# Moving operands that begin 12 bytes into their tiles, in a one-core decoder trunk

## The chip, the cores and the metric

The kernel runs on one core of a Trainium2 chip. The metric is the time of one execution on the device, in microseconds (us); lower is better. Before the change the median of three runs is 2180.16 us (2179.63 to 2182.27).

A core has TensorE (PE in the profile; PEld is its loading of weights), VectorE (DVE), ScalarE (ACT), GpSimd (POOL) and SyncE (SP), which here only issues transfers. A matmul has a stationary operand, the weights, which are loaded into the array first, and a moving operand, whose columns then stream through it.

## The reference

One layer of a decoder for 512 prompt tokens and 8 sample tokens, 520 columns in all, in fp32:

```
proj = rmsnorm(x) @ w_in            # 2048 -> 6160
mixer = [ short convolution of 3 taps, gated | 4 heads of gated linear attention ]
x = x + mixer @ w_out               # 2048 -> 2048
u, v = split(rmsnorm(x) @ w_up)     # 2048 -> 2 * 5632
x = x + (silu(conv3(u) + b) * v) @ w_down
y = rmsnorm(x)
```

The outputs are y for both kinds of token, the last rows of the convolutions and the states of the attention.

## The kernel before

Activations lie transposed: a tile has 128 features in its 128 partitions and the T = 520 tokens along the row. `halves(t)` cuts it into two moving operands of HT = 260 columns. The large products are computed in float32r, in parts that take a number apart: `hi` is the rounded value, `lo` what the rounding left. ScalarE makes `hi` and VectorE `lo`, for the activations (`split`, lines 121 to 124) and for the weights (`parts`, line 111, and `prepare`, lines 1179 to 1198). A product is three matmuls: hi by hi, hi by the activations' lo, lo by hi.

Three places issue nearly all matmuls:

- `mm3`, line 140, in the first stage (the input projection, tile by tile in `group` and `span`) and at the very end (the last four row tiles of `w_down`, where the columns are cut into 264 and 256 instead of 260 and 260);
- `up_product`, line 1218, for the rest of the input projection and for the FFN's up projection;
- `chunk_product`, line 1461, for `w_out` and `w_down`.

The last two use a scheme that makes a 2 by 2 block product from seven products instead of eight (`ORDER`, seven forms of the activations in `xq` and `xd`, and sums of weights made by VectorE and by accumulating transfers). Each of the seven has 24 matmuls of 260 columns, and 168 matmuls make one group. The loop at line 1668 goes through all products in order, prepares the weights two products ahead, and runs the steps of the gates, norms and stores by due times written into generators (`yield 4.5`: four and a half products later). `InOrder` ties every engine to the order in which the program is written.

The moving operands live in tiles of [128, 520] float32r, 2,080 bytes a row:

- `pair_tiles` (line 200) makes hi and lo tiles: the first stage's `xa`, form 1 of the FFN, and the last activations of `load_last` (line 1436);
- `load_form` (line 630) loads the seven forms of a chunk from DRAM, through SyncE's or GpSimd's queue;
- `form` (line 670) makes the FFN's forms on the chip; `load_sum` (line 1570) loads some of their sums.

Slots are named by tags, and tiles of other kinds share them: `place` in `mixer_sums` (line 699) and the sums `acc` (`new_sums`, line 1420).

Three more kinds of tile matter for the room in SBUF. `tmp` (line 92) gives eight temporaries of T + 2 columns. `keep_last` (line 582) collects the last rows of the convolutions into `last`, [128, 10, n] with n = 8 for the mixer and 11 for the FFN under two tags, transposes them and copies the result to `flat`, from which ten small transfers store them; `flat` has two buffers. `zpad` holds the convolutions' inputs with two columns of padding.

Of the kernel before, what the change touches and what calls it, by code (L numbers as in the profile page):

```python
# [9 lines left out]
F32 = mybir.dt.float32  # L10
F32R = mybir.dt.float32r
# [6 lines left out]
P = 128  # L18
# [4 lines left out]
T = NP + NS  # L23
# [14 lines left out]
def trunk_kernel(  # L38
# [13 lines left out]
    tp = ctx.enter_context(tc.tile_pool(name="tmp", bufs=8))  # L52
# [37 lines left out]
                self.last[i.engine] = i.name  # L90

    def tmp():
        return tp.tile([P, T + 2], F32, tag="t", name="t")

    def two(ap):
        return ap.rearrange("p (a b) -> p a b", a=2)
# [24 lines left out]
    def split(src, hi, lo, scale=None):  # L121
        if scale is None:
            nc.scalar.activation(hi, src, AF.Copy)
            nc.vector.tensor_tensor(lo, src, hi.bitcast(F32), op=ALU.subtract)  # L124
        else:
            nc.scalar.activation(hi, src, AF.Copy, scale=scale)
            nc.vector.scalar_tensor_tensor(
                lo, src, scale, hi.bitcast(F32), op0=ALU.mult, op1=ALU.subtract
            )

    def halves(t):
        return t[:, :HT], t[:, HT:T]
# [63 lines left out]
    bigA = actx.enter_context(tc.tile_pool(name="bigA", bufs=1, side="right"))  # L196
    bctx = ctx.enter_context(ExitStack())
    b12p = bctx.enter_context(tc.tile_pool(name="b12", bufs=1))

    def pair_tiles(pool, tag):  # L200

        return [pool.tile([P, T], F32R, tag=f"{tag[0]}{s}{tag[1:]}", name=tag[0] + s) for s in "hl"]

    xa, xw = [], {}
    for k in range(KD):
# [71 lines left out]
    with ExitStack() as es:  # L277
# [173 lines left out]
        for k in range(KD):  # L451
            c, t = k // 4, k % 4
# [117 lines left out]
    zp = actx.enter_context(tc.tile_pool(name="zpads", bufs=1, side="right"))  # L570
    yt1 = actx.enter_context(tc.tile_pool(name="yt1", bufs=1, side="right"))
# [4 lines left out]
    last = [None]  # L576
# [5 lines left out]
    def keep_last(z, j, n, new_p, new_s, get=None):  # L582

        jj = j % n
        if jj == 0:
            last[0] = zp.tile([P, 10, n], F32, tag=f"last{n}", name="last", bufs=2)
        if get:
            nc.scalar.activation(last[0][:, :, jj], z[:, NP:], AF.Copy)
        else:
            nc.gpsimd.tensor_copy(last[0][:, :, jj], z[:, NP:])  # L590
        if jj == n - 1:
            lt, c0 = last[0], (j - n + 1) * P

            def out():
                ps = (get or bank)()
                nc.tensor.transpose(
                    ps[: 10 * n, :P], lt.rearrange("p r j -> p (r j)"), idn
                )
                flat = zp.tile([110, P], F32, tag="flat", name="flat", bufs=2)
                nc.scalar.activation(flat[: 10 * n, :], ps[: 10 * n, :P], AF.Copy)  # L600
                for r in range(10):
                    dst = new_p[0, 0, r] if r < 2 else new_s[0, r - 2, 1]
                    (nc.gpsimd if get else nc.sync).dma_start(
                        dst[c0 : c0 + n * P].rearrange("(j p) -> j p", p=P),
                        flat[r * n : (r + 1) * n, :],
                    )

            soon.append(lambda: None)
            soon.append(out)

    def minus(out, ps, x):
        nc.vector.scalar_tensor_tensor(out, ps, -1.0, x, op0=ALU.mult, op1=ALU.subtract)
# [4 lines left out]
    def sub(out, x, y):  # L617
        nc.vector.tensor_tensor(out, x, y, op=ALU.subtract)
# [8 lines left out]
    slots = [None] * KD  # L627
    forms_d, xd = {"wo": g_d}, {}

    def load_form(kind, c, j):  # L630

        home = (7 * c + j) % 8
        if kind == "down" and home in (0, 7):
            home = 7 - home
        parts_ = []
        for x in range(2):
            tiles = []
            for q in range(2):
                t = slots[2 * home + q].tile(
                    [P, T], F32R, tag=f"y{'hl'[x]}{2 * home + q}", name="form"  # L640
                )
                pool = x == 1 if c == 0 else kind == "wo"
                (nc.gpsimd if pool else nc.sync).dma_start(
                    two(t.bitcast(F32)),
                    forms_d[kind][c][PLACE[ORDER[j]], x, 2 * q : 2 * q + 2].rearrange(
                        "i p c -> p i c"
                    ),
                )
                tiles += halves(t)
            parts_.append(tiles)  # L650
        xd[kind, c, ORDER[j]] = list(zip(*parts_))
# [11 lines left out]
    def acc_tag(n):  # L663
        return f"x{'hl'[n % 2]}{8 + n // 2}"
# [5 lines left out]
    def form(f, g):  # L670

        if f == 1:
            x = pair_tiles(bigA, f"b{g}")
        elif f in (2, 3):
            x = [
                bigA.tile([P, T], F32R, tag=acc_tag(4 * g + q), name="b2")
                for q in ((0, 3) if f == 2 else (1, 2))
            ]
        else:
            k = homes.get((f, g), {5: 0, 4: 4, 6: 8, 7: 12}[f] + g)  # L680
            x = [slots[k].tile([P, T], F32R, tag=f"y{s}{k}", name=f"y{s}{k}") for s in "hl"]
        for j, q in enumerate(zip(*(halves(y) for y in x))):
            xq[f, 2 * g + j] = q
        return x

    def first_tile(kind, g, m):

        return 4 * g + 2 * m if kind == "down" else 2 * g + 8 * m

    def rows_of(d, kind, g, q):  # L690

        m, b = first_tile(kind, g, q // 2), q % 2
        return d[m : m + 2, :, b * HT : (b + 1) * HT].rearrange("m p c -> p m c")

    def mixer_sums():

        def place(n):
            return yt1.tile([P, T], F32, tag=f"y{n}", name="yx")  # L700

        for g in (1, 2, 3, 0):
            xg = [place(n) for n in ("l0 h8 l8 h0" if g % 2 else "l1 l4 h4 h0").split()]
            for q, x in enumerate(xg):
                nc.sync.dma_start(two(x), rows_of(xT_d, "mix", g, q))
            yield
            for q, x in enumerate(xg):
                m = first_tile("mix", g, q // 2)
                for j, h in enumerate(halves(x)):
                    nc.scalar.activation(h, h, AF.Copy, scale=gmix[:, m + j : m + j + 1])  # L710
                if q == 1:
                    yield
            yield
            t1, t3, t4, b22 = xg
            t2 = place("h1")
            sub(t1, t1, t3)
            minus(t2, t1, b22)
            yield
            if g:
                for f, t in ((5, t1), (4, t2)):  # L720
                    nc.gpsimd.dma_start(mt_d[f - 4, g], t)
            sub(t3, b22, t3)
            minus(t4, t2, t4)
            yield
            nc.gpsimd.dma_start(mt_d[3, g], t4)
            if g:
                nc.gpsimd.dma_start(mt_d[2, g], t3)
        for f, t in ((5, t1), (6, t3), (4, t2)):
            split(t, *form(f, 0))
# [32 lines left out]
    with ExitStack() as mix:  # L762
# [44 lines left out]
        with ExitStack() as gl:  # L807
# [263 lines left out]
            for h in range(NH):  # L1071
# [3 lines left out]
                k = gp.tile([P, T], F32, tag="qk", name="k", bufs=5)  # L1075
# [3 lines left out]
                q = gp.tile([P, T], F32, tag="qk", name="q", bufs=5)  # L1079
# [6 lines left out]
                for d in range(2):  # L1086
                    ps = group(w_in, 4096 + h * DV + d * P, xa, None if h + d else v0)
                    t = gp.tile([P, T], F32, tag="v", name="v", bufs=2)
# [330 lines left out]

    def new_sums(g):  # L1420
        for q in range(4):
            acc[g, q] = bigA.tile([P, T], F32, tag=acc_tag(4 * g + q), name="acc")

    def load_residual(g):

# [21 lines left out]
    acc, dnp = {}, [None, None]  # L1447
# [55 lines left out]
    def projected(g):  # L1503
# [25 lines left out]
        def out(f, t):  # L1529

            if f == 7 or g == NG - 1:
                split(t, *form(f, g))
            else:
                nc.sync.dma_start(t_d[f - 4, g], t)
# [133 lines left out]
    for i, (kind, at, r) in enumerate(order):  # L1668
        j, n = i % 7, i // 7
# [41 lines left out]
        if i in (0, 2, NW, NW + 2):  # L1711

            x = xq[1, 0][0]
# [11 lines left out]
        if kind == "wo":  # L1725
            c, g = at
            if c == 0 and g == 2 and j == 0:
                load_form("wo", 1, 0)
            if c == 0 and j == 4 and g + 1 < NG:
                load_residual(g + 1)  # L1730
            if c == 0 and g == 2 and j == 1:
                add_residual("wo", 0)
            if c == 0 and g == NG - 1 and j >= 1:
                load_form("wo", 1, j)
            if c == 1 and g == NG - 1:

                for f, h in {
                    0: ((5, 0), (5, 1)), 2: ((5, 2),), 3: ((4, 0), (4, 1)), 4: ((4, 2),),
                    5: ((6, 0), (6, 1)), 6: ((6, 2),),
                }.get(j, ()):  # L1740
                    loaded.append(load_sum(t_d, f, h))
        if 7 * n in (NM - 7, NU - 7):
            for x in {1: (0, 1), 2: (2, 3), 4: (4, 5), 6: (6,)}.get(j, ()):
                load_form(groups[n + 1][0], 0, x)
        if i == NM:
            new_sums(0)
        if kind == "down":
            c, g = at
# [157 lines left out]
```

## Time and profile before

| | us |
|---|---|
| median of the runs before | 2180.16 |
| span of the profiled execution | 2180.4 |
| PE busy | 2152.9 (99%), 17,751 matmuls |
| PEld busy | 2131.3 (98%) |
| DVE busy | 1735.7 (80%) |
| ACT busy | 1114.0 (51%) |
| POOL busy | 438.1 (20%) |
| moved by DMA | 415.51 MB, mean 191 GB/s |
| mean granted TensorE clock | 0.995 |

The profiled execution's own time is its span, 2180.4 us, 0.2 us over the median. Matmuls are pipelined: one takes some 283 ns from its start to its modelled end, while the next starts much sooner. Sums of busy time therefore overlap, and it is the number of matmuls that start in a stretch which tells their pace. A line "A:B length, busy (xcount) ..." is a stretch of time with each engine's busy time and count.

### The profile page before, as it was taken

What the parts mean: (1) busy time and instruction counts of PE and PEld (TensorE: products, weight loads), DVE (VectorE), ACT (ScalarE), POOL (GpSimd) and SP (SyncE); (2) the same over time, 40 slices, a digit from 0 to 9 for tenths busy, and PEclk for the clock granted to TensorE, in tenths of its full rate; (3) what the DMA queues carried; (4) which work ended last, traced back from release to release, by engine and by line L of the source; (5) the groups of instructions that cost most, each with busy time, mean ns of one, the idle gap of its engine ahead of it and who ended that gap; (6) DMA issues with size and microseconds to landing.
All of it is one profiled execution on the core that took longest, in us unless ns stands there. A gap on an engine that the chain in (4) does not pass through costs nothing.

```text
span 2180.4 us, 43803 instructions
## 1 busy us (share of the span) xinstructions
PE 2152.9 (99%) x17751; PEld 2131.3 (98%) x17751; DVE 1735.7 (80%) x2298; ACT 1114.0 (51%) x1625; POOL 438.1 (20%) x625
## 2 busy tenths in 40 slices
PE   9999999999999999999999999999999999999997
PEld 8999999999999999999999999999999999999997
DVE  6346465578888897988888988998998778888886
ACT  6335435355544586555555555555555553444445
POOL 4213131121243321121221131122111310010000
PEclk9999999999999999999999999999999999999999
DMA  8545464387788996667676676676677886894734
GB/s 247 147 125 158 122 191 124 92 246 210 204 257 248 297 266 176 179 178 187 164 189 174 165 195 176 163 194 177 171 186 190 285 202 197 248 271 132 226 107 156
DMA packets 467163, 415.51 MB, mean 191 GB/s; under 512 B 21641, under 2 KB 426393, under 8 KB 466817
## 3 DMA queue, kind: packets, MB, share of 16 engines
q1 hardware_dynamic: 424081, 289.71, 46.5%
q0 software_dynamic: 42832, 122.93, 21.4%
q8 instruction: 139, 2.28, 0.4%
q14 instruction: 63, 0.52, 0.1%
q10 hardware_dynamic: 48, 0.07, 0.0%
HBM read 299.45 MB, written 80.31 MB: 174 GB/s over the span
## 4 chain that ended last, share of the span: by engine, by line
PE 88%; DMA 4%; DVE 3%; issue 1%; ACT 1%; POOL 1%; SPq 0%; ACTq 0%; DVEq 0%; POOLq 0%
PE mm L1218 34%; PE mm L140 16%; PE ms L1218 14%; PE y L1461 7%; PE x L1461 7%; PE f L1461 3%; PE e L1461 3%; PE ms L957 1%; DMA raw<-in_w_out_dram 1%; DMA form<-g_d 1%; DVE lo L1198 1%; DMA g_d<-fh 1%; DMA x_d<-acc 1%; DMA yl<-t_d 0%; DMA raw<-in_w_down_dram 0%
## 5 line engine op out<-in xcount | busy, mean ns | idle before, releaser
L1218 PE MATMUL mm<-yl,hi 128*128 128x260 f32 x1696 | 479.8, 283 | 3.6 <-DVE yl L124 3.6
L1218 PE MATMUL mm<-yh,hi 128*128 128x260 f32 x1696 | 480.5, 283 | 2.1 <-ACT ms L1228 1.8
L1218 PE MATMUL mm<-yh,lo 128*128 128x260 f32 x1696 | 479.8, 283 | 0.8 <-DVE lo L1198 0.8
L1194 ACT ACTIVATE hi<-raw 128x1024 fp32r<-128x1024 f32 x324 | 342.6, 1057 | 233.9 <-PE mm L1218 69.0
L1198 DVE TENSOR_TENSOR lo<-raw,hi 128x1024 fp32r<-128x1024 f32 x324 | 395.2, 1220 | 41.2 <-ACT hi L1194 40.7
L1198 DVE TENSOR_TENSOR lo<-s,hi 128x1024 fp32r<-128x1024 f32 x243 | 298.3, 1228 | 127.2 <-ACT hi L1194 121.9
L1194 ACT ACTIVATE hi<-s 128x1024 fp32r<-128x1024 f32 x243 | 256.9, 1057 | 217.2 <-DVE s L1139 80.2
L1218 PEld LDWEIGHTS mm<-yl,hi 128*128 128x128 f32 x1696 | 320.1, 189 | 4.2 <-DVE yl L124 4.2
L1218 PEld LDWEIGHTS mm<-yh,hi 128*128 128x128 f32 x1696 | 319.7, 189 | 2.7 <-ACT ms L1228 2.0
L1218 PEld LDWEIGHTS mm<-yh,lo 128*128 128x128 f32 x1696 | 320.4, 189 | 1.2 <-DVE lo L1198 1.2
L1218 PE MATMUL ms<-b,hi 128*128 128x260 f32 x1408 | 257.8, 283 | 0.0
L1218 PEld LDWEIGHTS ms<-b,hi 128*128 128x128 f32 x1408 | 218.5, 190 | 0.0
L1461 PE MATMUL x<-form,hi 128*128 128x260 f32 x1120 | 204.6, 283 | 0.8 <-DVE acc L1480 0.8
L1461 PE MATMUL y<-form,hi 128*128 128x260 f32 x1120 | 204.5, 282 | 0.5 <-DVE acc L1480 0.5
L1139 DVE TENSOR_TENSOR s<-s,raw 128x1024 f32<-128x1024 f32 x162 | 197.8, 1221 | 2.8
L1218 PE MATMUL ms<-b,lo 128*128 128x260 f32 x704 | 199.5, 283 | 0.0
L1461 PEld LDWEIGHTS x<-form,hi 128*128 128x128 f32 x1120 | 172.4, 188 | 1.2 <-issue 1.0
L1461 PEld LDWEIGHTS y<-form,hi 128*128 128x128 f32 x1120 | 172.5, 188 | 0.8 <-issue 0.7
L1461 PE MATMUL y<-form,lo 128*128 128x260 f32 x560 | 158.2, 283 | 0.8 <-DVE lo L1198 0.8
L1461 PE MATMUL x<-form,lo 128*128 128x260 f32 x560 | 158.1, 282 | 0.0
L112 DVE TENSOR_TENSOR lo<-raw,hi 128x1024 fp32r<-128x1024 f32 x76 | 93.7, 1238 | 78.2 <-ACT hi L111 71.6
L1218 PEld LDWEIGHTS ms<-b,lo 128*128 128x128 f32 x704 | 133.4, 190 | 0.0
(366 smaller groups left out, 5077.8 us busy)
## 6 DMA issues: line engine op xcount, KB each, us to landing
raw<-in_w_up_dram SPq DMA_DIRECT2D x176, 512.0 KB, 4.7
raw<-in_w_down_dram SPq DMA_DIRECT2D x96, 512.0 KB, 5.5
raw<-in_w_in_dram SPq DMA_DIRECT2D x92, 512.0 KB, 4.4
form<-f_d SPq DMA_DIRECT2D x126, 260.0 KB, 6.8
raw<-raw POOLq DMA_DIRECT2D x56, 512.0 KB, 5.5
f_d<-t POOLq DMA_DIRECT2D x80, 260.0 KB, 5.5
raw<-in_w_out_dram SPq DMA_DIRECT2D x32, 512.0 KB, 12.7
form<-g_d POOLq DMA_DIRECT2D x42, 260.0 KB, 7.7
```

The source lines that it names most:

```text
L112: nc.vector.tensor_tensor(lo, raw, hi.bitcast(F32), op=ALU.subtract)
L140: nc.tensor.matmul(o, w, xx, start=first and i == 0, stop=last and i == 2)
L957: nc.tensor.matmul(pb[:, c * 64 : (c + 1) * 64], L[:, c, :], rhs[:, c], start=True, stop=True,)
L1139: return lambda: nc.vector.tensor_tensor(out, x, y, op=ALU.add)
L1194: nc.scalar.activation(his[i], src, AF.Copy)
L1198: nc.vector.tensor_tensor(los[i], src, his[i].bitcast(F32), op=ALU.subtract)
L1218: nc.tensor.matmul(st["bank"][b], w[:, k, :], x, start=b not in st["used"] and k == 0 and j == 0, stop=k == 7 and j == 2, skip_group_check ...
L1461: nc.tensor.matmul(ps[:, m, :], w[:, k, m * P : (m + 1) * P], x, start=b not in st["used"] and k == 0 and j == 0, stop=k == 3 and j == 2, ...
```

## The change

A new helper `moving` makes a tile of T + 3 = 523 columns and returns it from column 3 on: the operand has 520 columns as before and begins 12 bytes into its tile. `pair_tiles`, `load_form` and `form` take their tiles from it. `place` and `new_sums`, which share the slots, make tiles of the same width and use the first 520 columns. To make room for three more columns per tile, `tmp` loses its two spare columns, `last` uses one tag of 110 columns for both sizes, and `flat` has one buffer. The instructions, their order and the transfers' shapes stay; the weights' tiles stay as they are.

```diff
     def tmp():
-        return tp.tile([P, T + 2], F32, tag="t", name="t")
+        return tp.tile([P, T], F32, tag="t", name="t")
...
+    def moving(pool, tag, name):
+
+        return pool.tile([P, T + 3], F32R, tag=tag, name=name)[:, 3:]
+
     def pair_tiles(pool, tag):
 
-        return [pool.tile([P, T], F32R, tag=f"{tag[0]}{s}{tag[1:]}", name=tag[0] + s) for s in "hl"]
+        return [
+            moving(pool, f"{tag[0]}{s}{tag[1:]}", tag[0] + s) for s in "hl"
+        ]
...
-            last[0] = zp.tile([P, 10, n], F32, tag=f"last{n}", name="last", bufs=2)
+            last[0] = zp.tile([P, 110], F32, tag="last", name="last", bufs=2)[:, : 10 * n]
+            last[0] = last[0].rearrange("p (r j) -> p r j", j=n)
...
-                flat = zp.tile([110, P], F32, tag="flat", name="flat", bufs=2)
+                flat = zp.tile([110, P], F32, tag="flat", name="flat", bufs=1)
...
-                t = slots[2 * home + q].tile(
-                    [P, T], F32R, tag=f"y{'hl'[x]}{2 * home + q}", name="form"
-                )
+                t = moving(slots[2 * home + q], f"y{'hl'[x]}{2 * home + q}", "form")
...
-                bigA.tile([P, T], F32R, tag=acc_tag(4 * g + q), name="b2")
+                moving(bigA, acc_tag(4 * g + q), "b2")
...
-            x = [slots[k].tile([P, T], F32R, tag=f"y{s}{k}", name=f"y{s}{k}") for s in "hl"]
+            x = [moving(slots[k], f"y{s}{k}", f"y{s}{k}") for s in "hl"]
...
-            return yt1.tile([P, T], F32, tag=f"y{n}", name="yx")
+            return yt1.tile([P, T + 3], F32, tag=f"y{n}", name="yx")[:, :T]
...
-            acc[g, q] = bigA.tile([P, T], F32, tag=acc_tag(4 * g + q), name="acc")
+            acc[g, q] = bigA.tile([P, T + 3], F32, tag=acc_tag(4 * g + q), name="acc")[:, :T]
```

## The prediction

> **What bounds the kernel now.** I read the page's first part, then the chain that ended last, then the matmul count per stretch, and last single matmuls in order of time.
>
> ```profile
> span 2180.4 us, 43803 instructions
> PE 2152.9 (99%) x17751; PEld 2131.3 (98%) x17751; DVE 1735.7 (80%) x2298; ACT 1114.0 (51%) x1625; POOL 438.1 (20%) x625
> ...
> PE 88%; DMA 4%; DVE 3%; issue 1%; ACT 1%; POOL 1%; SPq 0%; ACTq 0%; DVEq 0%; POOLq 0%
> ```
>
> TensorE is busy for 99% of the span and makes 88% of the chain. Busy alone says little, because one matmul overlaps the next. The distance from one start to the next is what counts, and the view of stretches gives it (columns: length; busy time and count of PE, PEld, DVE, ACT, POOL; clock; DMA share; GB/s):
>
> ```profile
> 600.00:700.00 100.00, 100.00 (x836) 100.00 (x836) 84.11 (x99) 48.90 (x65) 39.48 (x55) 1.00 0.86 251
> ...
> 1000.00:1100.00 100.00, 100.00 (x837) 100.00 (x837) 89.80 (x124) 55.25 (x82) 23.89 (x37) 1.00 0.67 174
> ...
> 2000.00:2100.00 100.00, 100.00 (x837) 100.00 (x837) 83.90 (x86) 42.08 (x45) 0.00 (x0) 1.00 0.52 159
> ```
>
> About two of the 837 stick out at the edges, so 835 start in 100 us: **0.1198 us apart**. It is the same with GpSimd at 39 us or at none and with the DMA share at 0.86 or at 0.52, at a full clock. So other engines and transfers don't set this pace; it is TensorE's own. Where it isn't kept is the passage into the FFN:
>
> ```profile
> 700.00:760.00 60.00, 60.00 (x500) 59.82 (x499) 50.74 (x55) 32.69 (x44) 25.44 (x35) 1.00 1.00 292
> 760.00:830.00 70.00, 64.17 (x501) 62.64 (x500) 66.83 (x83) 54.73 (x89) 12.59 (x16) 0.96 1.04 275
> ```
>
> There the DMA share is 1.00 and more, and between 760 and 830 us some 83 matmuls are missing against the pace (70 / 0.1198 = 584).
>
> How many matmuls does the change touch? Those of lines 140, 1218 and 1461 read the tiles that are moved:
>
> ```profile
> 0.00:2181.00 2181.00, 1074.78 (x8904) 0.99 0.68 191
> ...
> 0.00:2181.00 2181.00, 566.05 (x4704) 0.99 0.68 191
> ...
> 0.00:2181.00 2181.00, 426.22 (x3264) 0.99 0.68 191
> ```
>
> Together 8,904 + 4,704 + 3,264 = 16,872 of the 17,751. At 0.1198 us they make 2,021 us of the span, so **one nanosecond per matmul is worth 16.9 us**, 0.8%.
>
> **Is there anything to win in the 119.8 ns?** Four stretches of the order in time bear on it. Of plain fp32, with the same 260 columns (line 550), then 64 columns (line 957):
>
> ```profile
> 166.67 1.04 PE L550 MATMUL ms<-t,ones 128*128 128x260 f32 x4
> 133.43 1.00 PE L957 MATMUL ms<-L 128*128 128x64 f32 x8
> ```
>
> And how long one of each lasts (the mean in ns stands ahead of the idle time):
>
> ```profile
> L550 PE MATMUL ms<-t,ones 128*128 128x260 f32 x16 | 4.2, 382 | 0.0
> L957 PE MATMUL ms<-L 128*128 128x64 f32 x224 | 28.3, 269 | 1.0 <-DVE L L897 1.0
> ```
>
> One lasts 0.38 us at line 550 and 0.27 at line 957. So four starts at line 550 are (1.04 - 0.38) / 3 = 0.220 us apart. If float32r streams columns at twice that rate (an estimate, from 0.220 against 0.1198), its pass would need 0.110. The 64-column passes are (1.00 - 0.27) / 7 = 0.104 apart though they have a quarter of the columns, so what sets them is loading 128 columns of weights. Both bounds lie near 0.110 us; the kernel's pass takes 0.1198. **Some 9.8 ns per matmul are unexplained** by columns or by weights alone; they appear when both streams run at full rate. In time the two begin together:
>
> ```profile
> 1000.06 0.28 PE L1218 MATMUL mm<-yh,hi 128*128 128x260 f32 x1
> 1000.07 0.19 PEld L1218 LDWEIGHTS mm<-yl,hi 128*128 128x128 f32 x1
> ```
>
> Then the number of columns. At the end the batch is cut into 264 and 256 columns (first and last rows; 24 rows and 22 rows in all):
>
> ```profile
> 2112.62 0.28 PE L140 MATMUL mm<-bh,hi 128*128 128x264 f32 x1
> ...
> 2115.43 0.28 PE L140 MATMUL mm<-bh,lo 128*128 128x264 f32 x1
> ```
>
> ```profile
> 2149.03 0.28 PE L140 MATMUL mm<-bl,hi 128*128 128x256 f32 x1
> ...
> 2151.50 0.28 PE L140 MATMUL mm<-bl,hi 128*128 128x256 f32 x1
> ```
>
> 2.81 / 23 = 0.1222 us for 264, 2.47 / 21 = 0.1176 for 256, 0.1198 for 260 between: 4.6 ns for eight columns, more than a bare column time (0.110 / 260 x 8 = 3.4). The surplus grows with what is read. Four columns are 16 bytes; per 16 bytes the pass costs 119.8 / 65 = **1.84 ns**. I use that as the step in which a start can shift things.
>
> Last, does the start matter? A tile is 2,080 bytes and its second half begins 1,040 bytes in, so in a pool's line of tiles the halves begin alternately at a multiple of 32 bytes and 16 past it. Line 1461 takes six matmuls from one half, then six from the next:
>
> ```profile
> 2040.77 0.40 PE L1461 MATMUL e<-form,hi 128*128 128x260 f32 x2
> ...
> 2041.49 0.40 PE L1461 MATMUL e<-form,hi 128*128 128x260 f32 x2
> ...
> 2042.20 0.40 PE L1461 MATMUL e<-form,hi 128*128 128x260 f32 x2
> ...
> 2042.92 0.40 PE L1461 MATMUL e<-form,hi 128*128 128x260 f32 x2
> ```
>
> 0.72, 0.71 and 0.72 us: a start moved by 16 bytes changes nothing to 0.01 us in six, 1.7 ns in one. By the widths in the code, every operand of these three lines begins at a multiple of 16 bytes. The change puts all of them at 12 bytes past one, which no row shows.
>
> **The change part by part.**
>
> (1) The start of the moving operand, 16,872 times. From below: a gain cannot exceed the surplus, 119.8 - 110 = 9.8 ns each, 165 us. From above: a pass of 1,040 bytes that starts 12 bytes into a line touches 66 lines of 16 bytes where it touched 65; a line more at 1.84 ns is 31.0 us. Between these ends I take a gain, because the surplus is there, it appears only with two reads at full rate, and all starts, weights (slices of 512 bytes) and moving columns alike, now fall on the same 16-byte grid at the same instant (the two rows at 1000.06). Three columns of four move the columns' line changes away from those of the weights. Of its size I take one step of the grid, 1.84 ns, not the whole surplus, since the nearest row, the 16-byte shift, shows nothing and the two reads drift against each other when one is held up. 16,872 x 1.84 = 31.0 us.
>
> (2) The stretch 700 to 830 us waits for transfers; its 1,001 matmuls give nothing: 1,001 x 1.84 = 1.8 us less. **Sum: -29.2 us.**
>
> (3) Writers of the wider tiles. ScalarE and VectorE write the same elements 12 bytes further on. I cost that at nothing: VectorE is busy 89.8 of 100 us in the densest stretch and TensorE waits for neither there. A pass of 0.1180 instead of 0.1198 raises VectorE to 91% (89.8 x 0.1198 / 0.1180); with the whole surplus gone it would stand at 98% and begin to bind.
>
> (4) Transfers into the wider tiles (`load_form`, `load_sum`, `load_last`) land 12 bytes into a tile, in the same pieces. Those that the chain shows waited for are
>
> ```profile
> 712.37 7.03 DMA form<-g_d
> 719.91 7.50 DMA form<-g_d
> ...
> 809.67 10.59 DMA yl<-t_d
> ```
>
> 25.1 us in all; elsewhere a product's forms come a chunk ahead. Bounds: nothing, or half as long again, +12.6 us. The nearest row is the second half of each tile, already 16 past a multiple of 32 and no group of its own; I take nothing.
>
> (5) Room: `tmp` loses two columns nobody reads, `last` shares one tag, `flat` has one buffer. A `flat` is next written when its ten stores are out; these land in a median of 4.9 us and there are five uses, the first and the last 1,078 us apart.
>
> ```profile
> L600 ACT ACTIVATE flat<-mm x4: 273/278/280, 635.6 to 1495.0; 110x128 f32<-110x128 f32 x3, 80x128 f32<-80x128 f32 x1
> L600 ACT ACTIVATE flat<-f x1: 278/278/278, 1713.8 to 1713.8; 110x128 f32<-110x128 f32 x1
> ...
> DMA to landing us min/median/max: 1.6/4.9/5.9
> ```
>
> Nothing; without that cover it would be 5 x 4.9 us of ScalarE, which is half idle. Instructions, DMAs and their order stay.
>
> The profiled span is 2180.4 us and the median of the runs 2180.16, so the sum goes onto the latter: 2180.2 - 29.2 = **2151 us**.
>
> **The rivals.**
>
> *The whole surplus goes* (9.8 ns; 15,871 matmuls outside the waiting stretch): -155 us, 2025; VectorE, at 98%, would give some back, say 2040. For it: 0.110 is what both streams show alone. Against: a single shift must end every collision.
>
> *The start doesn't matter*: 2180. For it: the 16-byte shift. Against: it stays on the grid.
>
> *A line more is read*: slower. Each pass fetches 66 lines; place: lines 140, 1218, 1461; price 1.84 ns x 16,872 = 31 us, **2211**. It decides if the fetch of lines sets the pace: then 256, 260 and 264 columns should scale as 64, 65 and 66 lines, 117.9, 119.8 and 121.6; measured 117.6, 119.8 and 122.2. That is close, and the strongest point against my forecast.
> The Trainium skill, SBUF — State Buffer, Specifications, speaks for this rival: lines have 16 bytes, want at least two hits each for full bandwidth, and every crossing costs; the shifted operand's first line has one hit. By that rule the sum would be 2211 or a little more; the trace's growth with columns agrees with it, its 16-byte shift cannot test it.
>
> *Transfers to odd addresses slow down* in the passage: +12.6 us at unchanged matmuls, 2193. For it: share 1.00 there. Against: same bytes, same pieces.
>
> **How the numbers follow.** Chances: a gain of the order of a line step 0.40 (its own range 0.4 to 4 ns, 2117 to 2174); whole surplus 0.14; no change 0.18; a line more 0.20; slower transfers 0.08. A measurement of this kernel can tell about 0.2%, 4 us, from no change. Faster 0.54, same 0.18, slower 0.28. The range leaves out the lower half of the whole-surplus case and the tail above one line: 2050 to 2214.
>
> **What would show it.** Matmuls per 100 us in 1000 to 1100, the two at the edges counted in: 850 if I am right (100 / 0.118 + 2), 837 if the start doesn't matter, 824 with a line more, some 910 for the whole surplus. The cuts at the end should move alike (264 and 256 columns). I am wrong if that count stays and the time moves, or if 700 to 830 grows.

## The result: 0.3% faster, a fifth of what was forecast

| | before | after |
|---|---|---|
| median of the runs, us | 2180.58 (2179.63 to 2182.27, 6 runs) | 2174.7 (2173.31 to 2175.17, 6 runs) |
| ratio, 95% interval | | 0.997 (0.9959 to 0.9981) |
| span of the profiled execution, us | 2180.4 | 2173.3 |

The change makes the kernel 5.9 us faster by the medians, 7.1 us by the two spans. The forecast was 29. Later in the study the changed kernel was timed once more beside the kernel before: 2174.19 against 2180.25 us, ratio 0.9972 (0.9963 to 0.9981). Of the kernels timed below, the one with start 0 had one run among twelve at 2211.44 us and a granted clock of 0.928, where the others had 0.996 to 0.998; it lifts that kernel's ratio to 1.0026, where the medians give 1.0013.

The first part of the page after the change (span; busy time and share of each engine with its instructions) and the chain that ended last:

```profile
span 2173.3 us, 43803 instructions
PE 2142.5 (99%) x17751; PEld 2119.4 (98%) x17751; DVE 1735.1 (80%) x2298; ACT 1111.8 (51%) x1625; POOL 438.8 (20%) x625
...
PE 93%; DVE 3%; DMA 1%; issue 1%; ACT 1%; SPq 0%; POOL 0%; ACTq 0%; DVEq 0%; POOLq 0%
...
form<-f_d SPq DMA_DIRECT2D x126, 260.0 KB, 6.7
form<-g_d POOLq DMA_DIRECT2D x42, 260.0 KB, 7.5
```

As many instructions as before, on every engine. TensorE is busy 10.4 us less (2152.9 before), and the time outside it, span less busy, grew by 3.3 us (27.5 to 30.8): that is the 7.1. The last two rows are the loads into the moved tiles: 6.7 and 7.5 us from issue to landing.

The stretches of the changed kernel (columns: length; busy time and count of PE, PEld, DVE, ACT, POOL; granted clock; DMA share; GB/s). All but the first and the one of 1800 to 1900 us stand for the kernel before in the prediction; these two are shown for it first, then all for the changed kernel:

```profile
400.00:500.00 100.00, 97.20 (x783) 96.07 (x782) 65.72 (x97) 46.31 (x69) 16.39 (x24) 0.98 0.67 188
...
1800.00:1900.00 100.00, 98.40 (x819) 98.01 (x819) 82.52 (x84) 40.45 (x43) 4.82 (x4) 1.00 0.75 226
```

```profile
400.00:500.00 100.00, 95.69 (x779) 93.89 (x778) 66.31 (x97) 46.64 (x70) 16.44 (x24) 1.00 0.68 190
...
600.00:700.00 100.00, 100.00 (x842) 100.00 (x841) 84.54 (x99) 48.64 (x65) 40.12 (x56) 1.00 0.86 250
700.00:760.00 60.00, 59.78 (x500) 59.42 (x499) 51.13 (x56) 33.19 (x44) 24.95 (x34) 1.00 1.00 294
760.00:830.00 70.00, 64.47 (x501) 62.71 (x500) 66.73 (x82) 54.92 (x91) 12.74 (x15) 0.95 1.06 278
1000.00:1100.00 100.00, 100.00 (x840) 100.00 (x839) 90.20 (x124) 55.01 (x82) 24.69 (x37) 1.00 0.68 179
1800.00:1900.00 100.00, 97.20 (x815) 96.82 (x814) 83.53 (x84) 40.90 (x44) 4.83 (x4) 1.00 0.74 217
2000.00:2100.00 100.00, 100.00 (x843) 100.00 (x842) 84.34 (x85) 43.34 (x46) 0.00 (x0) 1.00 0.50 154
```

Between 1000 and 1100 us 840 matmuls stand where 837 stood, between 2000 and 2100 us 843. With the two at the edges left out, as the prediction did, the pace is 100 / 838 = 119.3 ns in the up projection and 100 / 841 = 118.9 in the chunk products, against 119.8 in both. The passage from 700 to 830 us holds 500 and 501 matmuls as before. (These 130 us are no fine measure: a second profile of the changed kernel has 1,019 matmuls there, at a granted clock of 1.00, where the first has 999 at 0.97.) So the pace moved the forecast way in both kinds of product, and the size is a quarter to a half of the step that was assumed.

The chain gives the same with a finer ruler. A piece of 96 matmuls of one group of the up projection, before and then after, the first and the last that the chain lists whole:

```profile
859.38 11.51 PE mm L1218 x96
...
1684.65 11.51 PE mm L1218 x96
```

```profile
856.61 11.44 PE mm L1223 x96
...
1679.42 11.44 PE mm L1223 x96
```

There are 41 groups of 168 matmuls from the first row to the last: (1684.65 - 859.38) / 41 = 20.13 us a group before, (1679.42 - 856.61) / 41 = 20.07 after, or 119.8 and 119.5 ns a matmul with what lies between the groups.

Where did the 3.3 us outside TensorE come from? The view of waits, for TensorE (us in total, times, longest), before:

```profile
PE mm L140 <- DVE bl L127: 1.1, 2, 0.9
...
PE mm L1218 <- DVE lo L1198: 0.8, 2, 0.5
...
PE y L1461 <- DVE lo L1198: 0.8, 1, 0.8
```

and after:

```profile
PE y L1466 <- DVE lo L1203: 2.0, 1, 2.0
...
PE mm L1223 <- DVE lo L1203: 1.6, 4, 0.8
PE mm L140 <- DVE bl L127: 1.6, 3, 0.9
```

These three grew from 2.7 to 5.2 us, 2.5 of the 3.3; a second profile of the changed kernel has 5.0. All three wait for a `lo` part that VectorE makes. The `lo` of the weights is waited for at two entries into a new run of products, near 460 and 1805 us: the rows of 400 to 500 us and of 1800 to 1900 us above, where TensorE stands still for 4.3 and 2.8 of 100 us instead of 2.8 and 1.6, 2.7 us more in all. The `bl` belongs to the first 25 us of the kernel. My reading of the two entries is that TensorE comes there earlier and finds VectorE's work no earlier by as much. No run changed VectorE's part to test it, but the slower kernels of the next section fit: these two waits for `lo` come to 0.3 us there with start 1, 1.5 with start 2 and 0.8 with start 0, where the change has 3.6. The `bl` doesn't fit: the kernel with start 1 waits 1.5 us for it, nearly as long as the change.

### The profile page after: what moved, and what is told of

The parts are those of the page before. It is cut to its first block, busy times and chain, and to the rows that moved or that the text cites. A ratio compares the mean times of both kernels' runs of the same rounds, so it can differ in the third digit from the quotient of the medians.

```text
span 2173.3 us, 43803 instructions
## 1 busy us (share of the span) xinstructions
PE 2142.5 (99%) x17751; PEld 2119.4 (98%) x17751; DVE 1735.1 (80%) x2298; ACT 1111.8 (51%) x1625; POOL 438.8 (20%) x625
## 4 chain that ended last, share of the span: by engine, by line
PE 93%; DVE 3%; DMA 1%; issue 1%; ACT 1%; SPq 0%; POOL 0%; ACTq 0%; DVEq 0%; POOLq 0%
PE mm L1223 34%; PE mm L140 15%; PE ms L1223 14%; PE y L1466 9%; PE x L1466 9%; PE e L1466 4%; PE f L1466 4%; PE ms L962 1%; DMA yl<-t_d 0%; DMA raw<-in_w_down_dram 0%; PE ms L948 0%; PE ms L1806 0%; SPq L1579 0%; DMA yl<-mt_d 0%; PE tp L306 0%
```

## The experiments

**Was it the start, or the room and the layout?** Three kernels keep everything of the change, tiles three columns wider and the savings of room, and move only the first column that is used: 0, 1 and 2 instead of 3.

```diff
-        return pool.tile([P, T + 3], F32R, tag=tag, name=name)[:, 3:]
+        return pool.tile([P, T + 3], F32R, tag=tag, name=name)[:, 0 : 0 + T]
```

(`1 : 1 + T` and `2 : 2 + T` in the other two.) In the built programs every one of these tiles begins at a multiple of 32 bytes; 523 columns take the room of 528. So the four starts are 0, 4, 8 and 12 bytes past a multiple of 16 bytes, in both halves of a tile.

> The changed kernel with its wider tiles, its room and its addresses, but every operand from column 0 of its tile. Theory of the start: the time goes back to before, 2180 (ratio 0.999 to 1.001), 837 matmuls per 100 us. Theory of the layout: it stays at 2175, 840 matmuls.

> The changed kernel with operands that begin one column, 4 bytes, into the tile. Theory of the start within 16 bytes: slower than before, by 1 to 2.5 ns per matmul, 2195 to 2220. Theory that any start off the 16-byte grid separates the two reads: 2175 as with three columns. Theory of the layout: 2175.

> The changed kernel with operands that begin two columns, 8 bytes, into the tile. Theory of the start within 16 bytes: slower than before, by 1 to 2.5 ns per matmul, 2195 to 2220. Any start off the grid, or layout: 2175.

The kernel before took 2179.9 us beside them. The stretches of 1000 to 1100 and of 2000 to 2100 us, with start 0, then 4 bytes, then 8:

```profile
1000.00:1100.00 100.00, 100.00 (x834) 100.00 (x833) 89.52 (x123) 54.89 (x81) 24.68 (x37) 1.00 0.68 179
2000.00:2100.00 100.00, 100.00 (x837) 100.00 (x836) 83.95 (x85) 41.46 (x45) 0.00 (x0) 1.00 0.51 159
```

```profile
1000.00:1100.00 100.00, 100.00 (x816) 100.00 (x815) 86.00 (x115) 52.56 (x77) 21.39 (x32) 1.00 0.66 173
2000.00:2100.00 100.00, 100.00 (x816) 100.00 (x815) 81.93 (x82) 40.79 (x44) 0.00 (x0) 1.00 0.58 178
```

```profile
1000.00:1100.00 100.00, 100.00 (x823) 100.00 (x823) 86.67 (x116) 52.52 (x77) 20.66 (x31) 1.00 0.66 171
2000.00:2100.00 100.00, 100.00 (x823) 100.00 (x823) 82.96 (x84) 41.71 (x45) 0.00 (x0) 1.00 0.55 171
```

| first column | bytes into the tile | ns per matmul at 1000 us | median us | ratio to before (95%) |
|---|---|---|---|---|
| 0 | 0 | 120.2 | 2182.79 | 1.0026 (1.0005 to 1.0048) |
| 1 | 4 | 122.9 | 2225.15 | 1.021 (1.0197 to 1.0223) |
| 2 | 8 | 121.8 | 2211.21 | 1.0147 (1.0134 to 1.016) |
| 3 (the result above) | 12 | 119.3 | 2174.7 | 0.997 (0.9959 to 0.9981) |

With the layout and the room of the change and the old start there is no gain, but a small loss of 2.9 us by the medians; at 1000 us the pace is 120.2 ns where the kernel before has 119.8. Why the layout costs that, no run shows. The whole gain comes from the 12 bytes. Against the right neighbour, start 0 on the same layout, they are worth more than the result shows: from all starts in the traces 120.2 became 119.4 ns at line 1218 and 120.0 became 119.0 at line 1461. Two of the three possible shifts make the kernel slower, one by 45 us, which is more than the 2195 to 2220 us expected for it. The transfers and the writers are shifted in these too, and the time goes with the pace of the matmuls.

**The pace by itself.** Three programs hold only streams of float32r matmuls with new weights for each, on tiles in SBUF, with nothing beside them. The first goes through starts of 0 to 15 columns, shifted weights, and widths from 128 to 512.

```diff
+    stream("from_a", 0)
+    stream("from_b", 1)
...
+    stream("from_p", 15)
...
+    stream("lena_a", 0, n=128, times=3)
...
+    stream("lenj_d", 3, n=512, times=3)
```

> Only streams of matmuls, nothing of the reference is computed: 96 float32r matmuls for each condition, weights changed for every one as in the kernel, the operand beginning 0 to 15 columns into a tile (from_a to from_p, back_a to back_d the first four again), then first and second halves by turns (halves_), then weights that begin 1 to 3 columns into their tile (wb_, wc_, wd_) under operands from column 0 (_xa) and 3 (_xd), then 128 to 512 columns from column 0 and 3 (len). Theory of the start: spacing of starts 119.8 ns from columns 0, 4, 8 and 12 and 0.5 ns less (119.3) from columns 3, 7, 11 and 15, the others between or lower. If it is the phase against the weights, weights from column 3 under operands from column 3 give 119.8 again, and weights from column 1 under operands from column 0 give 119.3. Theory of the layout: every start gives the same spacing to 0.2 ns, and the gain in the kernel came from where the tiles lie. If lines of 16 bytes set the pace, the spacing grows by 1.84 ns for four columns from 256 to 512; if the surplus is a fixed wait per matmul, by 1.69.

Its answer on starts was not clean. The same starts in the same order of operand tiles, run twice, gave two results. Start 1, then start 1 again later in the program (length of the program; busy time and count of this stream's matmuls; clock; DMA share; GB/s):

```profile
0.00:575.00 575.00, 12.38 (x96) 1.00 0.01 2
...
0.00:575.00 575.00, 11.68 (x96) 1.00 0.01 2
```

The same 96 matmuls take 12.38 or 11.68 us. Part of the difference is a slow beginning of the first one; with that left out the spacings, from all starts in the trace, are 124.1 and 120.0 ns. The two streams begin with different ones of the three weight tiles, but each tile takes its turn in both, and after the first turn the pace is 124.3 ns with every tile in the one and 120.0 with every tile in the other. So a short repeating sequence settles on one of several steady paces; 118.3, 120.0 and 123.3 ns come back in other streams. Start 3 gave 118.3 both times, start 0 118.7 and 118.6. So a short stream of this kind doesn't rank starts.

The widths did give a result. From column 0, with 128, 320, 384 and 512 columns:

```profile
0.00:575.00 575.00, 8.15 (x72) 1.00 0.01 2
...
0.00:575.00 575.00, 10.72 (x72) 1.00 0.01 2
...
0.00:575.00 575.00, 12.64 (x72) 1.00 0.01 2
...
0.00:575.00 575.00, 16.50 (x72) 1.00 0.01 2
```

One of them lasts 0.28, 0.31, 0.33 and 0.39 us in this trace, so the spacings are (busy - one) / 71: 111, 146.6, 173.4 and 226.9 ns. From 320 to 384 columns it is some 26.7 ns for 64, 0.417 a column. At that rate 512 columns would take 226.8 ns, which was measured, and at no columns at all some 13 ns would be left over. Not every width lies so well: 448 columns took 202.7 ns, 2.7 more than that line, and 512 columns from column 3 took 229.0. The later programs, with varied addresses, have 118.4 ns at 256 columns and 146.8 at 320 from column 0, 11.7 and 13.4 above 0.417 a column. **So the surplus is in the main a fixed wait per matmul, not one per 16 bytes.** The bound from weights alone, 111, is near the prediction's 110.

The second program takes the fixed sequence away: each start is run with many tiles and offsets, all at the same distance past a multiple of 16 columns, in four passes.

```diff
+                c = start + grid * (count[0] * 11 % 23 if grid == 16 else count[0] * 29 % 91)
```

> Only streams of matmuls again, nothing of the reference is computed. Each condition stands four times (the cuts of other widths twice), and within each its 32 operands begin at varied multiples of 16 columns plus the start, so that one address does not speak for all. Theory of the start within 16 bytes (from the first streams, 118.7 ns as the mean of starts 3, 7, 11 and 15, 119.4 of 0, 4, 8 and 12, 122 of the others): the order stays, three past a multiple of four lowest, by 0.3 to 1 ns under a multiple of four, the two others 1 to 3 ns above it. Theory of the address: the sixteen starts differ without an order in steps of four. Phase against the weights: under weights that begin one to three columns in, operands from column 3 lose their lead over operands from column 0.

The groups of this program (busy us, mean ns of one, idle). `from_i` to `from_l` begin 8, 9, 10 and 11 columns past a multiple of 16, which are 0, 1, 2 and 3 past a multiple of four; `from_h` begins 7 past it. In `wb`, `wc` and `wd` the weights begin one, two and three columns on, under start 0 (`xa`) and under start 3 (`xd`):

```profile
L74 PE MATMUL from_j<-x,w 128*128 128x260 f32 x384 | 47.6, 285 | 0.0
...
L74 PE MATMUL from_k<-x,w 128*128 128x260 f32 x384 | 47.3, 284 | 0.0
...
L74 PE MATMUL wd_xa<-x,w 128*128 128x260 f32 x384 | 46.9, 283 | 0.0
...
L74 PE MATMUL wb_xa<-x,w 128*128 128x260 f32 x384 | 46.8, 282 | 0.0
...
L74 PE MATMUL from_i<-x,w 128*128 128x260 f32 x384 | 46.6, 282 | 0.0
L74 PE MATMUL from_h<-x,w 128*128 128x260 f32 x384 | 46.6, 281 | 0.0
L74 PE MATMUL wc_xd<-x,w 128*128 128x260 f32 x384 | 46.5, 281 | 0.0
...
L74 PE MATMUL from_l<-x,w 128*128 128x260 f32 x384 | 46.2, 280 | 0.0
L74 PE MATMUL wd_xd<-x,w 128*128 128x260 f32 x384 | 46.1, 279 | 0.0
L74 PE MATMUL wb_xd<-x,w 128*128 128x260 f32 x384 | 46.0, 279 | 0.0
```

A group is four passes of 96, so the spacing is (busy - 4 x one) / 380: start 8 (`from_i`) 119.7 ns, start 9 (`from_j`) 122.3, start 10 (`from_k`) 121.5, start 11 (`from_l`) 118.6. Over all sixteen, worked out from the starts in the trace, the mean is 119.6, 123.3, 121.9 and 118.9 for 0, 1, 2 and 3 columns past a multiple of four. That is the kernels' order, and near their sizes. It is an order of means: among the four starts that are 3 past a multiple of four, 3, 11 and 15 take 118.6 to 118.8 ns, but start 7 takes 119.7 in each of its four passes and has no lead over starts 0, 4, 8 and 12 (119.1 to 119.9). The other widths of this program put 3 first too, and at 256 and 264 columns in the same order. At 258 and 262 columns, which are no multiple of four, the rest stand otherwise: at 262 start 0 is the slowest of the four, 122.3 ns against 121.7, 121.4 and 121.1 for starts 1, 2 and 3.

The shifted weights decide the prediction's reason. If the gain came from moving the columns' line changes away from those of the weights, then weights moved by one column or by three under an unmoved operand would win as much, and weights moved along with a moved operand (`wd_xd`) would lose it. Under start 0 weights moved by one, two and three columns give 120.2, 120.2 and 120.4 ns where unmoved ones give 119.6: no gain. Under start 3 they give 118.2, 119.3 and 118.4 where unmoved ones give 118.7: the lead stays, 0.9 to 2.0 ns with each of the four. So the weights' start has a small effect of its own, and **the lead is the moving operand's own start, not its phase against the weights.**

**Do the two halves, and wider operands, behave alike?** A product goes on from one half of a tile to the other, and the second half begins 260 columns on. The third program runs streams that alternate between two halves with 0, 4, 8 and 12 columns left free between them, from start 0 and from start 3, and starts 0 to 3 at 272 to 320 columns.

```diff
+                    name = f"{order}_{L[first]}_gap{L[gap]}"
+                    stream(name, first, first + 260 + gap, order=order, times=8 if order == "each" else 4)
```

> Only streams of matmuls, nothing of the reference is computed. Operands now change between a first half (from column 0, _a, or column 3, _d) and a second half that begins 260 columns on (gapa), or 264, 268 or 272 (gape, gapi, gapm), after three matmuls, after six, or at each, with tiles at varied multiples of 32 bytes; then widths of 272 to 320 columns from column 0 to 3. Theory that only the start within 16 bytes counts: all gaps alike to 0.3 ns, from column 3 lower than from column 0 by 0.9. Theory that a half that begins in the other 16 bytes of a 32-byte block costs something: gape and gapm (not 32 bytes apart in blocks, or apart, by the start) differ from gapa and gapi by 0.5 to 1 ns. Widths: if the start counts only where the weight load (111.7 ns for 128 columns) and the stream end close together, its four values join at 288 columns and above, at n x 0.4167 + 13.3 ns.

Groups of this program: the half changed at each matmul, from start 0 (`a`) and from start 3 (`d`), without a gap (`gapa`), with four columns (`gape`), and from start 3 with twelve (`gapm`); below them 320 columns from starts 0 to 3.

```profile
L93 PE MATMUL each_a_gape<-x,w 128*128 128x260 f32 x576 | 69.6, 282 | 0.0
L93 PE MATMUL each_d_gapa<-x,w 128*128 128x260 f32 x576 | 69.4, 281 | 0.0
L93 PE MATMUL each_d_gapm<-x,w 128*128 128x260 f32 x576 | 69.4, 281 | 0.0
L93 PE MATMUL each_a_gapa<-x,w 128*128 128x260 f32 x576 | 69.3, 282 | 0.0
...
L93 PE MATMUL each_d_gape<-x,w 128*128 128x260 f32 x576 | 68.8, 280 | 0.0
...
L93 PE MATMUL ne_b<-x,w 128*128 128x320 f32 x192 | 29.1, 312 | 0.0
L93 PE MATMUL ne_c<-x,w 128*128 128x320 f32 x192 | 28.8, 311 | 0.0
L93 PE MATMUL ne_a<-x,w 128*128 128x320 f32 x192 | 28.5, 309 | 0.0
L93 PE MATMUL ne_d<-x,w 128*128 128x320 f32 x192 | 28.3, 307 | 0.0
```

Four columns between the halves save nothing from start 0 (69.3 and 69.6 us) and save 0.6 us of 69.4 from start 3. By starts in the trace the pace from start 3 goes from 119.6 to 118.5 ns when the half changes at each matmul, from 119.1 to 118.5 at every third, from 119.3 to 118.7 at every sixth. With four free columns both halves begin 12 bytes past a multiple of 32 bytes; without them the second begins 28 past one, as in the changed kernel. But that isn't the rule: with twelve free columns both are 12 past a multiple of 32 as well, and 0.3 ns at most is saved (69.4 us; 119.6, 119.0 and 119.1 ns). So the distance of 264 columns is better than 260, 268 and 272, for a reason these runs don't show.

At 320 columns the spacings, (busy - 2 x one) / 190, are 146.7, 149.9, 148.3 and 145.7 ns for starts 0 to 3. The weights need only 111. The four starts were expected to join from 288 columns on; they don't. So the start matters where the columns set the pace and the weights have time to spare, and it doesn't need both reads at full rate, as the prediction had it.

**Put to use in the kernel.** If the streams carry over, the changed kernel leaves something at its second halves. In the next kernel a tile is 528 columns wide and its second half begins at column 267, 264 after the first; a second version has the same tiles and begins at 0 and 264.

```diff
-        return pool.tile([P, T + 3], F32R, tag=tag, name=name)[:, 3:]
+        return two(pool.tile([P, 528], F32R, tag=tag, name=name))[:, :, 3 : 3 + HT]
...
-            acc[g, q] = bigA.tile([P, T + 3], F32, tag=acc_tag(4 * g + q), name="acc")[:, :T]
+            acc[g, q] = bigA.tile([P, 528], F32, tag=acc_tag(4 * g + q), name="acc")[:, :T]
...
-        nc.sync.dma_start(x, d[f - 4, g])
+        nc.sync.dma_start(x, two(d[f - 4, g]))
```

(In the second version `[:, :, :HT]`.) Not shown are the helpers that take a tile in two pieces, and `load_last`: in both versions its tiles keep one piece from column 3, so the last four row tiles of `w_down` have the change's start even in the second one.

> The changed kernel, its tiles 528 columns wide (in the same room), the second half four columns further on, so that both halves begin 12 bytes past a multiple of 32 (columns 3 and 267). Theory from the streams that halves in the other 16 bytes of a 32-byte block cost something once the start is right: another 0.6 to 0.9 ns per matmul under the changed kernel, 118.4 to 118.7 ns, 2160 to 2166, ratio to before 0.991 to 0.994; 844 or 845 matmuls per 100 us. Theory that only the start within 16 bytes counts: 2175.

> The same with both halves at a multiple of 32 bytes, columns 0 and 264. From the streams: 119.8 to 120.0 ns with either distance, so 2180 to 2184. If what matters is that both halves begin alike: 2165 to 2172.

> The changed kernel once more on this chip, beside the two: ratio to before 0.996 to 0.998 by every theory.

The stretches of the version with starts 3 and 267:

```profile
1000.00:1100.00 100.00, 100.00 (x845) 100.00 (x845) 90.56 (x123) 55.23 (x82) 26.15 (x39) 1.00 0.69 184
2000.00:2100.00 100.00, 100.00 (x844) 99.91 (x843) 82.75 (x90) 43.67 (x46) 0.54 (x1) 1.00 0.52 160
```

and of that with starts 0 and 264:

```profile
1000.00:1100.00 100.00, 100.00 (x834) 100.00 (x833) 89.75 (x122) 54.31 (x82) 24.70 (x37) 1.00 0.67 175
2000.00:2100.00 100.00, 100.00 (x837) 100.00 (x836) 83.88 (x86) 41.54 (x45) 0.00 (x0) 1.00 0.51 159
```

| kernel, timed together | median us | ratio to before (95%) |
|---|---|---|
| before | 2180.25 | 1 |
| the changed kernel again: starts 3 and 263 | 2174.19 | 0.9972 (0.9963 to 0.9981) |
| starts 3 and 267 | 2165.16 | 0.9932 (0.9919 to 0.9946) |
| starts 0 and 264 | 2183.73 | 1.0018 (1.0009 to 1.0027) |

Starts 3 and 267 give 845 matmuls where the changed kernel has 840, 118.6 ns, and 9.0 us more than the change. Starts 0 and 264 give nothing. So the four columns between the halves help only together with the start, as in the streams, and this version beats both kernels. It shows that a distance of 264 is better than 260 here; it doesn't show why.

## Why the prediction was right and wrong

**What bounds the kernel: right.** The time went with TensorE's pace in all kernels. One nanosecond per matmul was put at 16.9 us. From start 0 to start 1 the pace moved by 122.9 - 120.2 = 2.7 ns and the medians by 42.4 us, 15.7 us per nanosecond; some of the 16,872 matmuls lie where TensorE waits for something else.

**Step (1), the start: right in direction, wrong in size, and the direction was luck.** The reason given for it would have had every start off the 16 bytes win, and two of the three lose. Three things were wrong in the step.

The size was "one step of the grid", 1.84 ns. Measured was 0.5 ns in the up projection and 0.9 in the chunk products. By line, from all starts in the trace: 0.41 x 8,904 = 3.7 us at line 1218, 0.85 x 4,704 = 4.0 at line 1461, 0.50 x 3,264 = 1.6 at line 140, together 9.3 us where 31.0 stood; TensorE's busy time, 10.4 us less, agrees. Part of the shortfall is the layout, which the prediction put at nothing: against start 0 on the same layout the start is worth 0.8 ns at line 1218 and 1.0 at line 1461, half of the step.

The step itself was no step. It divided the pace by 65 lines of 16 bytes and took "the surplus grows with what is read" from three widths at the end of the kernel. At 320, 384 and 512 columns from column 0 the surplus is some 13 ns; four columns cost 1.67 ns, and a start that costs a line needn't cost that. The 256 and 264 columns moved as the prediction asked only in part: from the starts in the trace 264 went from 122.0 to 120.5 ns, 256 stayed at 117.7 (with start 0 on the new layout they take 122.3 and 118.5).

The reason, line changes of columns and weights on the same grid at the same instant, is ruled out: 4 and 8 bytes leave the grid as 12 do and are slower; weights moved off the grid win nothing and lose nothing of the lead; at 320 columns, where the weights leave time to spare, the order of the starts is the same.

**Step (2), the passage: not refuted, but too narrow.** 700 to 830 us gave nothing, 500 and 501 matmuls in both, as far as a stretch can tell that differs by 20 matmuls between two profiles of one kernel. But it isn't the only place that waits. The two entries near 460 and 1805 us took back 2.7 us, more than the 1.8 that was deducted.

**Step (3), writers: nearly right.** VectorE's share went from 89.8 to 90.2 us in the densest stretch, and TensorE doesn't wait there. It does wait at the entries, for VectorE's `lo`: the cover that was named is missing just there. Waits for the weights' `lo` grew from 1.6 to 3.6 us.

**Steps (4) and (5), transfers and room: right for transfers, nearly for room.** Landing in 6.7 and 7.5 us where 6.8 and 7.7 stood, the same bytes, and with the old start on the new layout the gain is gone, so that none of it came from room. The new layout wasn't free either: 2.9 us by the medians.

**The rivals.** "The start doesn't matter" is refuted by the four starts, though the measured pace, 840, lies nearer to its 837 than to the forecast's 850. "The whole surplus goes" is refuted: 118.6 ns is the best pace of any kernel here, 111 the bound from the weights.

"A line more is read" is half true, and here the half counts that the prediction treated as one case. Starts 1, 2 and 3 all touch 66 lines where start 0 touches 65. Starts 1 and 2 cost 2.7 and 1.6 ns in the kernel, so these starts off the line do cost. The price of start 2 is near the 1.84 ns that was set. But start 3, with as many lines, is faster than start 0. The Trainium skill, SBUF — State Buffer, Specifications, says that lines have 16 bytes, want two hits each for full bandwidth, and that crossings cost. By it starts 1 and 3, which leave a single hit in the last line and in the first, should be the worst and alike, with start 2 between them and start 0; the trace agrees for starts 1 and 2 (122.9 and 121.8 ns against 120.2) and disagrees for start 3 (119.3). Neither the number of lines nor the hits in them decide.

**What stays open** is why 12 bytes win. No run shows what TensorE's reads do inside a line. The runs show an order, 3 before 0 before 2 before 1, at 256, 260, 264, 272, 288 and 320 columns; with 3 before 0 at every width from 256 to 320 that was run with varied addresses, and at 260 for every start of the weights. They don't show why start 7 has no lead, nor why the layout cost something; and they show that from start 3 alone the distance between the halves matters as well, where 264 columns are better than 260, 268 and 272.

## What to carry to other kernels

Where TensorE sets the pace with float32r matmuls, the first column of the moving operand within its 16 bytes is a knob worth 2.3% between its worst and its best place here (2225.15 and 2174.7 us); it is ranked by running a stream of matmuls over many tiles and offsets, since a short repeating sequence can settle on different paces. Look at every operand, not at the tile: where the second half begins was worth more here (9.0 us) than the change (6.1 us). And a surplus measured at three neighbouring widths should not be cut into steps: widths further apart tell a fixed wait from a price per line.

## What the runs showed of the hardware that was not expected

- Moving operands that begin 4 bytes past a multiple of 16 make float32r matmuls of 260 columns 2.7 ns slower than aligned ones (122.9 against 120.2 in the kernel), 8 bytes 1.6 ns slower (121.8), 12 bytes 0.9 ns faster (119.3), all against the aligned start on the same layout.
- From start 3 a second half 264 columns on instead of 260 saves a further 0.6 to 1.1 ns in the streams; from start 0 it saves nothing, and 268 and 272 columns save 0.3 ns at most from start 3.
- A float32r matmul with new weights takes 0.417 ns a column and some 13 ns more at 320, 384 and 512 columns (146.6, 173.4 and 226.9 ns), and 111 ns at the least, at 128 columns.
- A stream that repeats a short sequence of addresses keeps a steady pace, and the same operands at the same start can keep another one the next time (124.1 and 120.0 ns).
